# A prefix log-sum-exp kernel: half of its DMAs move from SyncE's queue to ScalarE's, and the last tile gets a stream of its own

## The chip, the cores and the metric

The kernel runs on one core of a Trainium2 chip. A core has five engines that run their own instruction streams and meet at semaphores: TensorE (PE in the profile; its weight loads are PEld), VectorE (DVE), ScalarE (ACT), GpSimd (POOL) and SyncE (SP). The data moves between HBM and the core's SBUF by 16 DMA engines, which an engine's instruction stream sets to work with a DMA instruction. The metric is the time of one execution on the device in microseconds (us); a lower time is better.

## The reference

For each of 4 batches and each of 4128 columns, a running log-sum-exp goes down 4096 rows:

```python
def setup_inputs():
    B, S, D = (4, 4096, 4128)
    return {'x': np.random.randn(B, S, D).astype(np.float32)}

def reference(x):
    B, S, D = x.shape
    out = np.zeros_like(x)
    out[:, 0, :] = x[:, 0, :].copy()
    for t in range(1, S):
        mx = np.maximum(out[:, t - 1, :], x[:, t, :])
        out[:, t, :] = mx + np.log(np.exp(out[:, t - 1, :] - mx) + np.exp(x[:, t, :] - mx))
    return out.astype(np.float32)
```

Row t of the output is log(exp(x[0]) + ... + exp(x[t])). All 270.5 MB of x are read once, and as many bytes of output are written.

## The kernel before, in words

**Tiles.** The rows of a batch are cut into tiles (class `Step`) of 128 x r rows and all 4128 columns. r is 3, but 32 blocks of 128 rows are not a multiple of 3, so one tile of each batch has r = 2: the first tile of batch 0, the last tile of the other three. That makes 11 tiles in each batch and 44 in all, numbered 0 to 43 here. Partition p of a tile holds r successive rows, so a tile of three rows is 128 x 12384 floats (6192 KB in the profile's DMA table), and one of two rows is 128 x 8256 (4128 KB). Tiles 0, 21, 32 and 43 are the small ones. Below, L43 is the load of tile 43 and S43 its store.

**Chunks.** A tile is computed in four chunks (class `Chunk`) of 1024 columns, and the last chunk carries the 32 columns that are left as a "tail" (tile `qt` in PSUM). For a chunk, ScalarE takes the exponential of all r rows at once (`exp`, line 142), in place, to fp16. TensorE then adds up along the partitions with triangular matrices (`head`, lines 92 and 96 through the helper `mm`): two matmuls with `incl` for row 0, two with `excl` for each further row, and, unless the tile is the first of its batch, two with `pick`, which add what the tile before has handed on in `carry`. `stage(j)` (line 175) takes the logarithm of the PSUM tile `pt` into row j of the tile (Ln), and two more matmuls with `ident` move `pt` on to row j + 1. After the last row `keep` (lines 106 and 107, VectorE) saves the carry of that chunk.

**Order.** The order of all instructions is written out by hand (`manual_schedule`). Iteration g of the main loop does the last stage of chunk g - 2, the middle stage of chunk g - 1 and the first of chunk g, then `exp` of chunk g + 2 and `head` of chunk g + 1. Chunks of successive tiles follow one another in this stream, so that `exp` for the first chunk of the next tile stands between the stages of the tile before.

**Buffers and DMAs.** Four tiles fit in SBUF (`xpool`, bufs = 4). The load (line 127) and the store (line 130) are issued by SyncE, whose stream has nothing else in it. When the last stage of tile k's last chunk has been done, SyncE issues S(k) and then L(k+3); that load goes into the buffer of tile k - 1 and waits until S(k-1) has landed. All DMAs lie in the one queue q1.

Of the kernel before, what the change touches and what calls it, by code (L numbers as in the profile page):

```python
# [11 lines left out]
R = 3  # L12
# [37 lines left out]
def kernel(  # L50
# [11 lines left out]
    nc = tc.nc  # L62
    B, S, D = x.shape
    assert S % P == 0
    n_main = D // CH
    tail = D - n_main * CH
    t0 = n_main * CH
    last = n_main - 1
# [5 lines left out]
    bufs = 4  # L74
# [37 lines left out]
    class Step:  # L112
# [7 lines left out]
            rows = t[self.b, self.row:self.row + P * self.r, :]  # L120
            return rows.rearrange("(p j) d -> p j d", j=self.r)

        def load(self):
            full = xpool.tile([P, R, D], FP32, name="xt")
            self.xt = full[:, :self.r, :]
            self.half = self.xt.bitcast(FP16)
            nc.sync.dma_start(out=self.xt, in_=self.dram(x))  # L127

        def store(self):
            nc.sync.dma_start(out=self.dram(out), in_=self.xt)  # L130

    class Chunk:
        def __init__(self, step, c):
# [51 lines left out]
    steps = []  # L185
# [8 lines left out]
            row += P * r  # L194
        assert row == S

    chunks = [Chunk(s, c) for s in steps for c in range(n_main)]
    ahead = bufs - 1
    for s in steps[:bufs]:
        s.load()  # L200
    stored = 0
    chunks[0].exp()
    chunks[1].exp()
    chunks[0].head()
    for g in range(len(chunks) + R - 1):
        for d in range(R - 1, -1, -1):
            if 0 <= g - d < len(chunks) and d < chunks[g - d].t.r:
                k = chunks[g - d]
                k.stage(d)
                if k.c == last and d + 1 == k.t.r:  # L210
                    k.t.store()
                    if bufs <= stored + ahead < len(steps):
                        steps[stored + ahead].load()
                    stored += 1
        if g + 2 < len(chunks):
            chunks[g + 2].exp()
        if g + 1 < len(chunks):
            chunks[g + 1].head()


# [28 lines left out]
```

## Time and profile before

| | |
|---|---|
| time, median of 3 runs | 1262.9 us (1262.69 to 1263.4) |
| span of the profiled execution, from its first to its last instruction | 1261.0 us |
| busy in that span: ACT / PE / DVE | 947.0 (75%) / 690.7 (55%) / 451.4 (36%) us |
| bytes moved, mean rate | 541.46 MB, 429 GB/s |
| share of the DMA engines' time in queue q1 | 99.4% |
| ScalarE's wait for loads (line 142) | 247.8 us, 42 times |

The profile is of one execution. Its span, 1261.0 us, is the execution's own time from first to last instruction; the measured times lie some 1.9 us above it. Busy times can overlap, since the engines work side by side; what bounds a kernel is read from the chain of work that ended last and from what each engine waited for. DMA-issuing instructions are not counted as busy. A DMA instruction's "time to landing" runs from its issue to the semaphore that reports that all of its bytes are there, so it includes the time in which the DMA stands in the queue behind others.

### The profile page before, as it was taken

What the parts mean: (1) busy time and instruction counts of PE and PEld (TensorE: products, weight loads), DVE (VectorE), ACT (ScalarE), POOL (GpSimd) and SP (SyncE); (2) the same over time, 40 slices, a digit from 0 to 9 for tenths busy, and PEclk for the clock granted to TensorE, in tenths of its full rate; (3) what the DMA queues carried; (4) which work ended last, traced back from release to release, by engine and by line L of the source; (5) the groups of instructions that cost most, each with busy time, mean ns of one, the idle gap of its engine ahead of it and who ended that gap; (6) DMA issues with size and microseconds to landing.
All of it is one profiled execution on the core that took longest, in us unless ns stands there. A gap on an engine that the chain in (4) does not pass through costs nothing.

```text
span 1261.0 us, 6165 instructions
## 1 busy us (share of the span) xinstructions
PE 690.7 (55%) x2268; PEld 236.3 (19%) x2268; DVE 451.4 (36%) x445; ACT 947.0 (75%) x733; POOL 2.2 (0%) x13
## 2 busy tenths in 40 slices
PE   3666545565565555555346655555534755555562
PEld 1222111121121111111112221211211211111120
DVE  2443333333333333334424333333442433333344
ACT  5997777777777777778569777777866977777784
POOL 0000000000000000000000000000000000000000
PEclk9987787877777777878778777777777778787776
DMA  9999999999999999999999999999999999999998
GB/s 411 411 443 428 432 429 437 431 431 434 437 429 431 431 439 431 434 427 434 436 431 433 434 431 438 430 434 432 435 431 433 437 430 434 433 434 431 433 420 348
DMA packets 12702, 541.46 MB, mean 429 GB/s; under 512 B 1408, under 2 KB 1408, under 8 KB 1408
## 3 DMA queue, kind: packets, MB, share of 16 engines
q1 hardware_dynamic: 12672, 541.07, 99.4%
q8 instruction: 18, 0.29, 0.1%
q14 instruction: 12, 0.10, 0.0%
HBM read 270.53 MB, written 270.53 MB: 429 GB/s over the span
## 4 chain that ended last, share of the span: by engine, by line
DMA 72%; ACT 19%; PE 5%; issue 2%; DVE 1%; SPq 0%; ACTq 0%
DMA xt<-in_x_dram 67%; ACT xt L142 10%; ACT xt L175 9%; DMA out_dram<-xt 5%; PE pt L96 3%; PE pt L92 2%; DVE carry L106 0%; DVE carry L107 0%; ACT xt L180 0%; SPq L130 0%; ACTq L244 0%; SPq L127 0%; ACTq L142 0%; PE qt L92 0%
## 5 line engine op out<-in xcount | busy, mean ns | idle before, releaser
L142 ACT ACTIVATE xt<-xt 128x3072 f16<-128x3072 f32 (+3 forms) x176 | 478.2, 2717 | 247.9 <-DMA xt<-in_x_dram 247.8
L175 ACT ACTIVATE xt<-pt 128x1024 f32<-128x1024 f32 x512 | 487.3, 1029 | 2.5 <-PE pt L96 0.7
L106 DVE CAST carry<-pt 32x1024 f16<-32x1024 f32 x176 | 216.5, 1230 | 760.9 <-ACT xt L175 760.7
L92 PE MATMUL pt<-xt,ident 128*128 128x512 f16 x176 | 76.6, 435 | 493.7 <-ACT xt L175 493.7
L96 PE MATMUL pt<-xt,ident 128*128 128x512 f16 x496 | 203.7, 477 | 35.4 <-ACT xt L175 34.7
L107 DVE TENSOR_TENSOR carry<-pt,carry 32x1024 f16<-32x1024 f32 x176 | 215.8, 1226 | 6.1
L96 PE MATMUL pt<-xt,excl 128*128 128x512 f16 x496 | 187.6, 496 | 0.0
L96 PEld LDWEIGHTS <-ident 128*128 128x128 f16 x496 | 51.0, 103 | 655.0 <-issue 641.3
L92 PE MATMUL pt<-xt,incl 128*128 128x512 f16 x176 | 92.2, 524 | 23.5 <-ACT xt L142 15.1
L92 PE MATMUL pt<-xt,excl 128*128 128x512 f16 x176 | 93.4, 531 | 0.0
L96 PE MATMUL pt<-xt,incl 128*128 128x512 f16 x176 | 92.9, 528 | 0.0
L96 PEld LDWEIGHTS <-excl 128*128 128x128 f16 x536 | 66.6, 124 | 104.1 <-issue 79.5
L92 PE MATMUL pt<-carry,pick 128*128 128x512 f16 x160 | 72.0, 450 | 0.0
L96 PE MATMUL pt<-carry,pick 128*128 128x512 f16 x160 | 68.5, 428 | 0.0
L180 ACT ACTIVATE xt<-qt 128x96 f32<-128x96 f32 (+1 forms) x44 | 10.9, 248 | 46.3 <-PE pt L96 46.3
L92 PEld LDWEIGHTS <-incl 128*128 128x128 f16 x220 | 22.6, 103 | 118.0 <-DVE carry L107 95.3
L92 PEld LDWEIGHTS <-excl 128*128 128x128 f16 x220 | 26.8, 122 | 36.8 <-issue 27.9
L96 PEld LDWEIGHTS <-incl 128*128 128x128 f16 x260 | 27.8, 115 | 10.9 <-issue 4.8
L92 PEld LDWEIGHTS <-pick 128*128 128x128 f16 x200 | 22.9, 114 | 30.4 <-issue 20.4
L96 PEld LDWEIGHTS <-pick 128*128 128x128 f16 x160 | 18.4, 115 | 28.6 <-issue 17.2
L92 PEld LDWEIGHTS <-ident 128*128 128x128 f16 x176 | 19.2, 109 | 22.7 <-issue 12.8
L106 DVE CAST carry_t<-qt 32x32 f16<-32x32 f32 x44 | 8.7, 197 | 26.0 <-ACT xt L180 25.8
(21 smaller groups left out, 56.5 us busy)
## 6 DMA issues: line engine op xcount, KB each, us to landing
xt<-in_x_dram SPq DMA_DIRECT2D x40, 6192.0 KB, 42.2
out_dram<-xt SPq DMA_DIRECT2D x40, 6192.0 KB, 28.1
xt<-in_x_dram SPq DMA_DIRECT2D x4, 4128.0 KB, 37.3
out_dram<-xt SPq DMA_DIRECT2D x4, 4128.0 KB, 29.6
```

What stands on the lines that cost most here:

```text
L92: nc.tensor.matmul(pt, lhsT=w, rhs=rhs, start=start, stop=stop, skip_group_check=True)
L96: pe.add_instruction(mybir.InstMatmult(name=nc.get_next_instruction_name(), ins=[pe.lower_ap(rhs), pe.lower_ap(w, for_matmul_weights=True) ...
L106: nc.vector.tensor_copy(cr[HI:HI + 32, :], pt[HI:HI + 32])
L107: nc.vector.tensor_tensor(out=cr[LO:LO + 32, :], in0=pt[HI:HI + 32], in1=cr[HI:HI + 32, :], op=mybir.AluOpType.subtract,)
L142: nc.scalar.activation(self.t.half[:, :, 2 * c0:2 * c0 + w], self.t.xt[:, :, c0:c0 + w], ACT.Exp,)
L175: nc.scalar.activation(t.xt[:, j, c * CH:(c + 1) * CH], pt, ACT.Ln)
L180: nc.scalar.activation(t.xt[:, :, t0:D], self.qt, ACT.Ln)
```

## The change

Three things change. (1) `load` and `store` are given the queue on which they are issued. Stores of tiles 0 to 21 and the loads that follow them (up to L24) are issued by SyncE as before; stores of tiles 22 to 43 and loads L25 to L43 are issued by ScalarE, out of the same instruction stream as its `exp` and Ln. (2) On ScalarE the load L(k+3) isn't issued right after S(k) but two iterations of the main loop later (`due[g + 2]`); it comes after the stages of that iteration and before its `exp`. On SyncE it stays in the same iteration. (3) The main loop runs twice: over the chunks of tiles 0 to 42 first, to the end of their last stages, and then over the four chunks of tile 43, which thus no longer stand between the stages of tile 42.

```diff
+        def load(self, queue):
...
-            nc.sync.dma_start(out=self.xt, in_=self.dram(x))
-
-        def store(self):
-            nc.sync.dma_start(out=self.dram(out), in_=self.xt)
+            queue.dma_start(out=self.xt, in_=self.dram(x))
+
+        def store(self, queue):
+            queue.dma_start(out=self.dram(out), in_=self.xt)
...
+    half = len(steps) // 2
+    stored = 0
+    due = {}
+    queue = lambda: nc.sync if stored < half else nc.scalar
     for s in steps[:bufs]:
-        s.load()
...
+        s.load(nc.sync)
+
+    for run in (steps[:-1], steps[-1:]):
+        chunks = [Chunk(s, c) for s in run for c in range(n_main)]
+        chunks[0].exp()
+        chunks[1].exp()
+        chunks[0].head()
+        for g in range(len(chunks) + R - 1):
+            for d in range(R - 1, -1, -1):
+                if 0 <= g - d < len(chunks) and d < chunks[g - d].t.r:
+                    k = chunks[g - d]
+                    k.stage(d)
+                    if k.c == last and d + 1 == k.t.r:
+                        k.t.store(queue())
+                        if bufs <= stored + ahead < len(steps):
+                            due[g if stored < half else g + 2] = (steps[stored + ahead], queue())
+                        stored += 1
+            if g in due:
+                s, q = due.pop(g)
+                s.load(q)
+            if g + 2 < len(chunks):
+                chunks[g + 2].exp()
+            if g + 1 < len(chunks):
+                chunks[g + 1].head()
+    assert not due
```

The removed loop is the same with `k.t.store()` and, right after it, `steps[stored + ahead].load()`, over the chunks of all tiles at once.

More of the change, by code (lines that the diff above doesn't have):

```diff
@@ L121, in dram @@
             return rows.rearrange("(p j) d -> p j d", j=self.r)
-        def load(self):
+        def load(self, queue):
             full = xpool.tile([P, R, D], FP32, name="xt")
@@ L195 @@
         assert row == S
-    chunks = [Chunk(s, c) for s in steps for c in range(n_main)]
     ahead = bufs - 1
+    half = len(steps) // 2
+    stored = 0
+    due = {}
+    queue = lambda: nc.sync if stored < half else nc.scalar
     for s in steps[:bufs]:
-        s.load()
[L201 to L218, printed above, removed]
+        s.load(nc.sync)
[22 more added lines that the diff above has]
+    assert not due
 _INS = ['x']
```

## The prediction

> **What bounds the kernel now.** I read the page first: the slices, the queues, the chain of work that ended last.
>
> ```profile
> DMA  9999999999999999999999999999999999999998
> q1 hardware_dynamic: 12672, 541.07, 99.4%
> DMA 72%; ACT 19%; PE 5%; issue 2%; DVE 1%; SPq 0%; ACTq 0%
> L142 ACT ACTIVATE xt<-xt 128x3072 f16<-128x3072 f32 (+3 forms) x176 | 478.2, 2717 | 247.9 <-DMA xt<-in_x_dram 247.8
> ```
>
> The DMA engines are busy in every slice, and ScalarE, the busiest compute engine, waits 247.8 us for loads: about 5.6 us in each of 44 tiles. The kernel is bound by its DMAs, and one queue suffices. Next, the DMA share by stretches; the last two columns are share and GB/s:
>
> ```profile
> 1180.00:1210.00 30.00, 16.53 (x56) 5.66 (x55) 10.21 (x10) 22.70 (x18) 0.00 (x0) 0.79 1.00 430
> 1226.00:1228.00 2.00, 2.00 (x7) 0.76 (x6) 0.46 (x3) 1.53 (x2) 0.00 (x0) 0.50 0.80 347
> 1228.00:1230.00 2.00, 0.68 (x3) 0.18 (x2) 0.54 (x1) 2.00 (x3) 0.00 (x0) 0.94 0.57 248
> 1230.00:1232.00 2.00, 1.28 (x4) 0.29 (x3) 1.92 (x2) 2.00 (x3) 0.00 (x0) 0.91 0.29 124
> 1232.00:1234.00 2.00, 2.00 (x6) 0.73 (x6) 0.00 (x0) 2.00 (x3) 0.00 (x0) 0.50 0.09 33
> 1234.00:1236.00 2.00, 0.89 (x3) 0.25 (x2) 1.96 (x2) 2.00 (x3) 0.00 (x0) 0.74 0.93 396
> ```
>
> In the steady part nothing is left (1.00). The only hole is at the end: S41 runs out engine by engine from 1226 to 1234, and S42 comes only then; 2 x (0.20 + 0.43 + 0.71 + 0.91 + 0.07) = 4.6 us of all engines. The timeline of SyncE dates S42 and S43, that of ScalarE the last tile, whose first `exp` starts when L43 has landed:
>
> ```profile
> 1234.00 0.33 SPq L130 DMA_DIRECT2D out_dram<-xt  x1
> 1244.51 0.33 SPq L130 DMA_DIRECT2D out_dram<-xt  x1
> ...
> 1216.53 2.86 ACT L175 ACTIVATE xt<-pt 128x1024 f32<-128x1024 f32 x3
> 1220.72 1.91 ACT L142 ACTIVATE xt<-xt 128x2048 f16<-128x2048 f32 x1 [1.34 <-DMA xt<-in_x_dram]
> 1243.46 1.02 ACT L175 ACTIVATE xt<-pt 128x1024 f32<-128x1024 f32 x1
> ```
>
> **Part 1: 22 stores and 19 loads issued by ScalarE.** On SyncE they cost 0.33 us and 0.38 us: 22 x 0.33 + 19 x 0.38 = 14.5 us, spread over 22 tiles, 0.7 us each. The wait for loads (5.6 us a tile) hides it, except for the last three (L43, S41, S42), after which ScalarE has no idle time to give: 1.0 us on the path. ScalarE's rows have no DMA issue; the bounds are 0.33 and the longest on SyncE, 1.5 us. I take SyncE's usual values: it is the same instruction. SyncE's queue loses what followed S21; nobody waits behind it.
>
> **Part 2: the loads two iterations later.** Stores land after 28.1 us (median) and tiles are 29.3 us apart, so when L(k+3) comes up S(k-1) has landed, and ScalarE does not block on it. L(k+3) now stands behind ScalarE's wait for L(k+2), then one `exp`, three Ln and the small Ln: by ScalarE's rows around L24's landing, 677.02 to 683.45, 6.4 us. In that time the DMA engines have S(k), which takes 14.65 us (half of 29.3). 8.2 us of it are left, so the queue never empties. The small tile 32 shortens its store to 9.75 us; its following load is issued before ScalarE's wait, since its last stage comes an iteration earlier. Cost in the steady part: nothing; the cover is the store ahead in the queue, and if it were gone each load would bring a gap of some 6 us.
>
> **Part 3: the change of queue.** S22 (668.50) goes to a new queue while L24 still runs in the old one (issued 638.10, 38.8 us to landing: 676.9). Before, S22 came behind it; now both have data at once. L24 lands later, ScalarE waits for it, and L25 stands behind that wait. S22 landed 23.1 us after issue, at 691.6; the last byte moves some 1.8 us earlier (S42, alone in the queue, took 16.4 us to landing, 14.65 of them transfer), at 689.8. L25 must be issued by 689.0 at the latest to start then (S42's bytes move from about 0.8 us after issue), so L24 must land by 682.6. If S22 were wholly first, L24 would land at 691.6: a gap of 9 us. If L24 keeps its place, none. With equal shares from 669.3 the 5.8 us of L24 that are left (to 675.1) take 11.6: it lands at 682.7, a gap of 0.1. Between 0 and 9 I take 0.5, as equal shares are nearest to a queue that all engines serve alike.
>
> No row shows two queues with data at once. The Trainium skill ("DMA: Bandwidth & Descriptors", section "Queues, rings and completion order") says that each engine takes turns between the queues that have work, a packet at a time. By that alone the gap would be the 0.1 us of equal shares, and the sum 0.4 us lower; no run here shows it yet.
>
> **Part 4: the last tile in its own stream.** Before, ScalarE ended three Ln at 1219.39 and went on with the last tile, interleaved with the stages that were left of tile 42. Now those come first. ScalarE reaches this point 0.71 us later (L43, S41): 1220.1. Then: two Ln and the wait for the last chunk's `head` (2.1 us of matmuls, 1220.13 to 1222.24 before) 2.85; its Ln 1.02; the wait before the small Ln 1.10 and itself 0.15; two Ln 1.95; two `ident` matmuls 0.9; the last Ln 1.02; S42's issue 0.4. Sum 9.4: S42 leaves at about 1229.1, 4.9 us earlier, but tile 43 begins at 1229.5, 8.8 us later than 1220.72. L43 has long landed.
>
> How long does tile 43 take alone? The nearest row is tile 0, the other two-row tile that runs by itself:
>
> ```profile
> 13.13 3.85 ACT L142 ACTIVATE xt<-xt 128x2048 f16<-128x2048 f32 x2 [11.05 <-DMA xt<-in_x_dram]
> 16.99 1.02 ACT L175 ACTIVATE xt<-pt 128x1024 f32<-128x1024 f32 x1
> ...
> 18.07 0.59 PE L92 MATMUL pt<-xt,ident 128*128 128x512 f16 x1 [1.11 <-ACT xt L175]
> 18.45 0.63 PE L96 MATMUL pt<-xt,ident 128*128 128x512 f16 x1
> ```
>
> Its matmuls start 0.43 us apart, half speed (0.22 in fast stretches, as at 1240). Tile 0 has no `pick`; tile 43 has two more matmuls per chunk. First Ln: 16.99 - 13.13 + 0.85 + 1.02 = 5.75. Then, per chunk, 0.06 + 7 x 0.43 + 0.63 + 0.02 + 1.02 = 4.75, three times; the small matmuls 0.25; at the end `ident`, small Ln and Ln 2.3: 22.55 us. At full speed ScalarE sets the pace: 4.9, twice 3.8, 3.2, 1.8: 17.5. I take 22.05: half speed as in tile 0, with only the last matmuls fast after the longest run of them.
>
> The Trainium skill ("TensorE: Matmul & The Clock Gate", Part 1) lets the clock double after a window of about 3.4 us of sustained work. The runs here would be 3.6 us with gaps of 1.1, so by that rule the clock could rise after any of them, and the stream take about 19.5 to 22: a sum up to 2.5 us lower than mine.
>
> So S43 is issued at 1229.5 + 22.05 + 0.05 = 1251.6 (1244.51 before). By then S42 is through (S41 landed at 1235.6, 14.65 more: 1250.2), so S43 runs alone: S42's 16.4 less a third of the transfer, 4.9: 11.5; landed 1263.1. From S43's landing (1244.51 + 15.7 = 1260.2) to the end the span had 0.8 more: 1263.9. With part 3: **1264.4** against the span of 1261.0. The measured median lies 1.9 above this span: **1266.3 us**, 0.27% slower.
>
> **Rivals.**
> *No measurable change.* The last tile's clock rises early: S43 at 1229.1 + 17.5 + 0.05 = 1246.6. Then the DMAs set the end: S42 through at 1250.2, S43 9.75 more, 0.8: 1260.8, with part 3 1261.3, time 1263.2. Up to 21.1 us for the stream the time stays under 1265.4. For it: TensorE ran fast in 1236 to 1244. Against it: that stretch had interleaved work; tile 0 had none and stayed slow.
> *The change of queue stalls* (slower): S22 goes first, 9 us more: 1275. It decides from about 2.5 us on. Against it: nothing here favours one queue.
> *Faster.* The hole of 4.6 us is filled, since S42 comes before S41 has run out: 1258.3. It needs S43 by 1245, that is, a stream of 15.5 us, below my full-speed sum, and that engines which finish S41 early set the end; the last one, at 1234, had no hole.
>
> **How the numbers follow.** A measurement of this kernel tells about 0.2% (2.5 us) from no change. Chances: forecast 0.45 (1265.4 to 1268), no change 0.40 (1262.5 to 1265.4), stall 0.09, faster 0.06; slower together 0.54. The range goes from the DMA bound, 1262.3, to 1270: the full 22.55, and issues on ScalarE at 1.5 us for the last three (3.5 more).
>
> **What would show it.** Part 1: DMA rows on ACT's queue near 0.35 us; ScalarE's waits for loads shorter by about 0.7 us a tile in the second half. Part 2: DMA share 1.00 from 700 to 1220; loads land some 23 us after issue (29.3 - 6.4) instead of 42.2. Part 3: one long wait of ScalarE, 5 to 8 us, near 677, and at most a short dip in DMA share near 690. Part 4: S42 near 1229, first `exp` of tile 43 just after it, S43 near 1251, no hole at 1228 to 1234 but one of 1 to 3 us before S43. I am wrong if the steady share falls below 0.99, if the dip at 690 exceeds 3 us, or if the last stream takes under 20 us.

## The result and the profile after

The changed kernel takes 1265.79 us (median of 13 runs, 1264.95 to 1266.52), the kernel before 1262.85 us in the same series (13 runs, 1262.45 to 1263.4): 2.9 us more, a ratio of 1.0023 with a 95% interval of 1.0015 to 1.0031. The forecast was 1266.3. The profiled execution has a span of 1263.6 us and a time of 1265.36, a little under the median.

The page of the changed kernel shows the two queues and a weak spot in the middle; the 22nd and 23rd of the GB/s slices are 404 and 414, and the DMA line's tenths don't show it:

```profile
span 1263.6 us, 6086 instructions
DMA  9999999999999999999999999999999999999998
GB/s 410 412 439 432 428 436 430 434 430 436 427 436 433 436 427 436 434 430 435 429 432 404 414 435 427 430 435 433 432 430 434 430 435 434 429 437 433 429 435 362
q1 hardware_dynamic: 6768, 289.56, 53.2%
q10 hardware_dynamic: 5904, 251.51, 46.3%
```

The table by stretches (last two columns: DMA share, GB/s) puts it at the change of queue. The first fence is of the kernel before, the second of the changed one:

```profile
686.00:694.00 8.00, 5.18 (x14) 1.73 (x14) 3.98 (x4) 8.00 (x8) 0.00 (x0) 0.79 0.98 423
700.00:1220.00 520.00, 288.51 (x947) 98.45 (x946) 184.33 (x181) 391.20 (x302) 0.00 (x0) 0.77 1.00 433
1226.00:1236.00 10.00, 6.85 (x19) 2.21 (x18) 4.88 (x7) 9.53 (x10) 0.00 (x0) 0.72 0.54 230
```

```profile
686.00:694.00 8.00, 4.92 (x13) 1.62 (x13) 3.83 (x5) 6.75 (x7) 0.00 (x0) 0.67 0.69 262
700.00:1220.00 520.00, 289.23 (x957) 101.42 (x956) 184.75 (x181) 399.27 (x305) 0.00 (x0) 0.78 1.00 431
1226.00:1236.00 10.00, 3.79 (x10) 1.12 (x9) 5.30 (x6) 7.49 (x7) 0.00 (x0) 0.73 0.95 411
```

At 686 to 694 the engines move 262 GB/s instead of the 431 of the steady part: 8 x (1 - 262/431) = 3.1 us are lost. In the 520 us after it, with all DMAs on ScalarE, the share is 1.00 as before (431 GB/s against 433). At the end the hole of 1226 to 1236 is gone, as S42 now waits in the queue; yet the time didn't fall.

ScalarE's timeline at the change of queue, in the changed kernel, shows how the gap comes about:

```profile
668.23 0.38 ACTq L130 DMA_DIRECT2D out_dram<-xt  x1
682.31 2.76 ACT L142 ACTIVATE xt<-xt 128x3072 f16<-128x3072 f32 x1 [6.09 <-DMA xt<-in_x_dram]
684.98 2.83 ACT L175 ACTIVATE xt<-pt 128x1024 f32<-128x1024 f32 x3
688.91 0.25 ACT L180 ACTIVATE xt<-qt 128x96 f32<-128x96 f32 x1 [1.10 <-PE pt L96]
688.91 0.35 ACTq L127 DMA_DIRECT2D xt<-in_x_dram  x1
```

S22 goes out at 668.23 on the new queue. ScalarE then waits 6.09 us for L24, which lands at 682.2 instead of 676.9; `exp`, three Ln and the small Ln follow, and only then L25 is issued, at 688.91. S22 landed 23.1 us after its issue, at 691.4.

And the end, in the changed kernel (ScalarE's timeline):

```profile
1198.05 2.76 ACT L142 ACTIVATE xt<-xt 128x3072 f16<-128x3072 f32 x1 [5.30 <-DMA xt<-in_x_dram]
1230.33 0.34 ACTq L130 DMA_DIRECT2D out_dram<-xt  x1
1230.71 3.85 ACT L142 ACTIVATE xt<-xt 128x2048 f16<-128x2048 f32 x2 [0.41 <-ACT xt L175]
1248.78 1.02 ACT L175 ACTIVATE xt<-pt 128x1024 f32<-128x1024 f32 x1
1249.83 0.34 ACTq L130 DMA_DIRECT2D out_dram<-xt  x1
```

L42's tile starts at 1198.05, 1.9 us later than before: two thirds of the whole loss are there before the last tiles begin. Tile 43 alone took 1249.83 - 1230.71 = 19.1 us. S42 needed 22.8 us to land (at 1253.1), S43 13.0 (at 1262.8): 9.7 us apart, the bare transfer of a small tile. By the trace's single packets the engines finished S42 one after another, from 1248.2 to 1252.6, and S43's first packets came at 1250.7. On the engines that were last S43 so still stood behind S42: there the DMAs set the end, not ScalarE.

### The profile page after: what moved, and what is told of

It is laid out like the page before. It is cut to its first block, busy times and chain, and to the rows that moved or that the text cites. A ratio compares the mean times of both kernels' runs of the same rounds, so it can differ in the third digit from the quotient of the medians.

```text
span 1263.6 us, 6086 instructions
## 1 busy us (share of the span) xinstructions
PE 688.2 (54%) x2268; PEld 239.0 (19%) x2268; DVE 451.4 (36%) x445; ACT 951.7 (75%) x733; POOL 2.2 (0%) x13
## 4 chain that ended last, share of the span: by engine, by line
DMA 71%; ACT 20%; PE 6%; issue 1%; DVE 1%; SPq 0%; ACTq 0%
DMA xt<-in_x_dram 69%; ACT xt L142 11%; ACT xt L175 9%; PE pt L96 4%; DMA out_dram<-xt 2%; PE pt L92 2%; ACT xt L180 0%; DVE carry L106 0%; DVE carry L107 0%; SPq L130 0%; ACTq L130 0%; SPq L127 0%; ACTq L127 0%; ACTq L142 0%; PE qt L92 0%
## 5 line engine op out<-in xcount | busy, mean ns | idle before, releaser
L92 PE MATMUL pt<-xt,ident 128*128 128x512 f16 x176 | 78.3, 445 | 499.0 <-ACT xt L175 498.8
L96 PE MATMUL pt<-xt,ident 128*128 128x512 f16 x496 | 205.2, 482 | 36.7 <-ACT xt L175 36.5
L107 DVE TENSOR_TENSOR carry<-pt,carry 32x1024 f16<-32x1024 f32 x176 | 215.8, 1226 | 6.1
## 6 DMA issues: line engine op xcount, KB each, us to landing
xt<-in_x_dram SPq DMA_DIRECT2D x23, 6192.0 KB, 42.2
xt<-in_x_dram ACTq DMA_DIRECT2D x17, 6192.0 KB, 22.7
```

What stands on the lines that cost most here:

```text
L92: nc.tensor.matmul(pt, lhsT=w, rhs=rhs, start=start, stop=stop, skip_group_check=True)
L96: pe.add_instruction(mybir.InstMatmult(name=nc.get_next_instruction_name(), ins=[pe.lower_ap(rhs), pe.lower_ap(w, for_matmul_weights=True) ...
L107: nc.vector.tensor_tensor(out=cr[LO:LO + 32, :], in0=pt[HI:HI + 32], in1=cr[HI:HI + 32, :], op=mybir.AluOpType.subtract,)
```

## The experiments

Two causes were possible in the changed kernel: the change of queue and the last stream. A third reading was a small price on each issue by ScalarE. All differences below are between medians, against runs of the kernel before on the same chip (1262.8 to 1262.9 us), unless another kernel is named.

**1. The change of queue alone.** Against the changed kernel:

```diff
-    for run in (steps[:-1], steps[-1:]):
+    for run in (steps,):
```

> The queue changes at tile 22 as in the change, but tile 43 stays in one stream with the others. Theory G (a gap at the change of queue: L24 and S22 share the engines, ScalarE waits for L24, and L25 stands behind that wait): 1.5 to 2.8 us above the kernel before, with the DMA share under 0.6 between 686 and 690 us and 1.00 from 700 us on. Theory P (each issue on ScalarE costs a little, 2.9 us / 22 tiles = 0.13 us a tile): 2.9 us, and no dip. Theory T (the last tile's own stream costs it): 0.

Measured: 1265.89 us, +3.0 us (ratio 1.0023, interval 1.0014 to 1.0032). Its table by stretches (last columns: DMA share, GB/s):

```profile
686.00:694.00 8.00, 4.71 (x13) 1.58 (x13) 3.84 (x5) 6.75 (x7) 0.00 (x0) 0.71 0.68 250
700.00:1220.00 520.00, 288.20 (x957) 101.16 (x956) 184.75 (x181) 398.89 (x305) 0.00 (x0) 0.78 1.00 432
```

8 x (1 - 250/431) = 3.4 us lost there; from 700 us on the share is 1.00. The whole loss of the change is in its queue part. It is a little above what theory G gave (1.5 to 2.8), and the share of 686 to 690 was 0.65, where under 0.6 was expected.

**2. The last stream alone.** Against the changed kernel:

```diff
-    queue = lambda: nc.sync if stored < half else nc.scalar
+    queue = lambda: nc.sync
...
-                            due[g if stored < half else g + 2] = (steps[stored + ahead], queue())
+                            due[g] = (steps[stored + ahead], queue())
```

> All DMAs on SyncE as before; only tile 43 has its own stream. Theory G: 0 to 1.2 us above the kernel before, as S43 is issued late (near 1248 us) but stands behind S42 in the queue anyway. Theory P: 0. Theory T: about 2.9 us, with a hole in the DMA share just before S43.

Measured: 1262.83 us, 0.0 us (ratio 1.0001, 0.9992 to 1.0010). S42 left at 1228.2 and landed 22.4 us later, at 1250.6; S43 left at 1248.0 and landed 12.3 us later, at 1260.3, 9.8 after S42. The hole only moved, from before S42 to before S43: the DMA share of 1226 to 1236 rose from 0.54 to 0.95, and that of 1236 to 1250 fell from 1.01 to 0.71. Theory T falls with this run, and theory P, which had no dip, with the first.

**3. L25 ahead of the wait.** Against kernel 1:

```diff
-                            due[g if stored < half else g + 2] = (steps[stored + ahead], queue())
+                            due[g if stored <= half else g + 2] = (steps[stored + ahead], queue())
```

> As the kernel that changes the queue alone, but L25, the first load on ScalarE's queue, is issued in the same iteration as S22, ahead of ScalarE's wait for L24; all later loads keep their two iterations. Theory G: the gap goes, -0.3 to 0.8 us against the kernel before, though L24 still lands some 6 us late. Theory P: still 2.9 us. A third reading, that sharing the engines between two queues itself wastes time: still about 2 us.

Measured: 1262.91 us, +0.05 us (1.0000, 0.9991 to 1.0009). ScalarE's timeline of this kernel, then a stretch with its DMA share:

```profile
668.58 0.38 ACTq L130 DMA_DIRECT2D out_dram<-xt  x1
669.06 3.79 ACTq L127 DMA_DIRECT2D xt<-in_x_dram  x1
682.64 2.76 ACT L142 ACTIVATE xt<-xt 128x3072 f16<-128x3072 f32 x1 [4.01 <-DMA xt<-in_x_dram]
```

```profile
686.00:694.00 8.00, 5.20 (x12) 1.63 (x12) 3.75 (x5) 6.90 (x8) 0.00 (x0) 0.61 1.00 429
```

L24 lands as late as in kernel 1 (682.6), and the engines are full: to within the interval, about 1.1 us either way, sharing them between two queues costs nothing in itself, and the whole loss goes with the gap behind ScalarE's wait.

**4. All DMAs on ScalarE.** Kernel 1 with `nc.scalar` for every load and store and `due[g + 2]` throughout.

> All DMAs on ScalarE's queue from the first load on, all loads two iterations later, one stream of chunks: no change of queue in flight. Theory G: only the activation table's load (1.28 us), which stands ahead of the first load on ScalarE, is lost: 0.9 to 1.7 us above the kernel before, and tiles 29.3 us apart. Theory P: that and 41 loads and 44 stores at half of 0.13 us each, 5.5 us more: about 6.9 us.

Measured: 1262.54 us, -0.3 us (0.9997, 0.9988 to 1.0006): not different. No price per issue shows; for all 88 together it is under 0.8 us by the interval. The 1.3 us at the start weren't lost either, a miss of mine; ScalarE's timeline there:

```profile
0.80 1.28 ACT L70 ACT_TABLE_LOAD   x1 [0.80 <-PEq L242]
0.84 1.94 ACTq L127 DMA_DIRECT2D xt<-in_x_dram  x4
```

The loads go out while the table load runs. Loads landed 22.8 us after issue in this kernel (42.2 before), and nothing was lost by that.

**5. The change of queue at tile 16.** Kernel 1 with another place:

```diff
-    half = len(steps) // 2
+    half = 16
```

> As the kernel that changes the queue alone (3.0 us above the kernel before), but at tile 16, far from a small tile. S16 then finds nearly all of L18 still to come: issued at 496.1, bytes from 496.9, L18's last byte 1.8 us before its landing at 509.9, so 11.2 us are left. Theory G with equal shares: L18 lands at 496.9 + 22.4 + 1.8 = 521.1, L19 is issued 6.6 us later and moves from 528.5, S16's bytes are through at 522.7: a gap of 5.8 us. 5.5 to 7.5 us above the kernel before. Rival (the first use of a second queue has a fixed price): 3.0 us again.

Measured: 1269.88 us, +7.1 us (1.0057, 1.0044 to 1.0069), inside theory G's range and far from the rival's. ScalarE's timeline of this kernel, then a stretch with its DMA share:

```profile
496.31 0.38 ACTq L130 DMA_DIRECT2D out_dram<-xt  x1
520.71 2.76 ACT L142 ACTIVATE xt<-xt 128x3072 f16<-128x3072 f32 x1 [16.41 <-DMA xt<-in_x_dram]
527.32 0.35 ACTq L127 DMA_DIRECT2D xt<-in_x_dram  x1
```

```profile
518.00:528.00 10.00, 2.65 (x7) 0.85 (x7) 2.83 (x4) 6.04 (x6) 0.00 (x0) 0.50 0.31 134
```

L18 landed at 520.7 (expected from equal shares: 521.1). 10 x (1 - 134/431) = 6.9 us are lost. By this theory tile 22, behind the small tile 21, was a cheap place: at S22's issue L24 was 8.7 us from the landing that it had before, L18 at S16's 13.6.

**6. L25 later still.** Kernel 1 with `g + 3` for that one load:

```diff
-due[g if stored < half else g + 2]
+due[g if stored < half else g + 3 if stored == half else g + 2]
```

> As the kernel that changes the queue alone, at tile 22, but L25 alone is issued three iterations after S22 instead of two. An iteration of ScalarE takes 5.4 us there. Theory G: 5.4 us more than with two iterations, 8.4 us above the kernel before (7.5 to 9.0). Rival (fixed price): 3.0 us.

Measured: 1268.09 us (1267.34 to 1270.43), +5.3 us (1.0045, 1.0032 to 1.0057). 8.4 was expected; the miss is in how far the issue moved. ScalarE's timeline of this kernel:

```profile
689.17 2.75 ACT L142 ACTIVATE xt<-xt 128x3072 f16<-128x3072 f32 x1
691.29 0.35 ACTq L127 DMA_DIRECT2D xt<-in_x_dram  x1
691.83 2.84 ACT L175 ACTIVATE xt<-pt 128x1024 f32<-128x1024 f32 x3
```

L25 left at 691.29, 2.4 us later than in kernel 1 (688.87) and not 5.4: it went out while the `exp` of 689.17 was running and before the three Ln that stand ahead of it in the program. For 2.4 us of delay the time rose by 1268.09 - 1265.89 = 2.2 us.

**7. The queues the other way round.** Kernel 1 with ScalarE first (`due[g + 2]`) and SyncE from S22 on (`due[g]`):

> The queues the other way round: ScalarE issues up to tile 21, SyncE the rest, one stream of chunks. The queue changes at the same place, but L25 stands on SyncE, which has nothing else to wait for. Theory G: no gap, -0.5 to 0.5 us against the kernel before, though L24 lands some 5 us late. Rival (fixed price of a change of queue): 3.0 us.

Measured: 1263.35 us, +0.5 us (1.0006, 0.9997 to 1.0015), at the edge of what was expected and not clear of no change. L24 landed at 682.3, L25 was issued on SyncE at 668.83, and 686 to 694 ran at 429 GB/s. A change of queue as such has no price near 3 us.

**8. A longer last stream.** Kernel 2, with the Ln of tile 43's second row done twice (the second writes the same values again):

```diff
-            nc.scalar.activation(t.xt[:, j, c * CH:(c + 1) * CH], pt, ACT.Ln)
+            for _ in range(2 if t is steps[-1] and j else 1):
+                nc.scalar.activation(t.xt[:, j, c * CH:(c + 1) * CH], pt, ACT.Ln)
```

> All DMAs on SyncE and tile 43 in its own stream, the four Ln of its second row done twice: up to 4 us more in the stream, some of it in ScalarE's waits for matmuls (2.6 us). S43 comes 1.5 to 4 us later than the 1248.0 of the kernel with the stream alone, where it just met the end of S42 (landed 1250.6, last byte about 1248.8). It then finds an empty queue: 1.0 to 4 us above that kernel. If there were slack behind S42: 0.

Measured: 1264.16 us (1262.99 to 1265.91), +1.3 us against kernel 2. S43 left at 1250.63 in the profiled run, 2.6 us later than in kernel 2, and landed 11.1 us after; S42 had landed at 1250.3. So S43 does become the bound once it is issued later than about 1248; the stream of the change lies at that edge.

**9. The change, with L25 ahead of the wait**, as in 3:

> The change as it is, with the last tile's own stream, but L25 issued in the same iteration as S22, ahead of ScalarE's wait for L24. Theory G, with the last stream free of cost: -0.5 to 0.5 us against the kernel before, and DMA share 0.95 or more in 686 to 694. If the last stream costs something once the gap is gone: about 1 us or more.

Measured: 1263.38 us (1262.54 to 1264.49), +0.6 us (1.0004, 0.9995 to 1.0013); the DMA share of 686 to 694 was 1.00. Without the gap S42 landed at 1250.3 and S43, issued at 1250.8, found an empty queue (11.1 us to landing; the profiled execution took 1264.4 us, 1 us above the median). What is left, if it is not noise, is probably this; no run shows it by itself.

**10. The change of queue at tile 16, with L19 ahead of the wait:**

> The change of queue at tile 16 (7.1 us above the kernel before), with L19 issued in the same iteration as S16. Theory G: the gap before L19 goes. L18 still lands at about 520.7, some 11 us late, so S17, behind it in ScalarE's stream by 16 us, is issued near 536.8 and moves from 537.6, where L19, behind S16 (through at 522.7), ends at 537.3 on the last engine and some 2 us earlier on the mean one: 0.5 to 2.5 us above the kernel before. Rival (the late landing itself costs): still 5 us or more.

Measured: 1264.34 us, +1.5 us (1.0013, 1.0004 to 1.0022), as expected. L18 lands just as late (520.8), S17 left at 536.61, and the stretch up to it, 528 to 536, is thin. The kernel's table there:

```profile
518.00:528.00 10.00, 2.59 (x7) 0.77 (x7) 2.77 (x4) 6.13 (x6) 0.00 (x0) 0.50 1.04 451
528.00:536.00 8.00, 6.17 (x18) 2.06 (x17) 2.54 (x3) 8.00 (x6) 0.00 (x0) 0.71 0.90 390
```

No kernel beat the one before beyond its interval.

## Why the prediction was right, and where it was not

The time (1266.3 against 1265.79), the sign and the size were right. Their make-up was not: the change of queue had 0.5 us and cost 3.0, the last stream had 2.9 and cost 0.0. That the sum came out is luck: two errors, one too small by 2.5 us and one too large by 2.9, cancelled. Two of the prediction's own signs of being wrong came true as well: the dip at 690 was 3.1 us by the table (limit 3), and the last stream took 19.1 us (limit 20).

**Part 1 was right.** The DMA rows on ScalarE's queue are 0.34 to 0.38 us long, and its waits for loads absorb them: in 700 to 1195 they fell from 102.1 to 85.8 us, 17 waits each, 1.0 us a tile where 0.7 was forecast. Kernel 4 shows no price either.

**Part 2 was right.** DMA share 1.00 from 700 to 1220; loads landed 22.7 us after issue (23 forecast).

**Part 3 named the mechanism and mis-sized it.** L24's landing by equal shares was forecast at 682.7 and came at 682.2. L25 left 6.7 us after it, at 688.9, where 689.0 was the limit worked out. By this the gap was 0.1, and I took 0.5; it cost 3.0 (kernel 1). The step that failed is the end of S22: I took its last byte on the last engine, 689.8, as the moment from which time is lost. The trace's single packets of the changed kernel tell what happened instead. The engines finished S22 one after another, from 686.4 to 690.9, and most of them then stood idle until L25's first bytes at 689.9, 1.0 us after its issue; and those first packets, on all engines at once, took 1.9 to 2.9 us instead of 1.83. Over the 16 engines this makes 2.1 us of idle time in the mean and 0.75 us of slow packets, 2.8 us in all.

So the loss is read from the bytes not moved, over all engines, and this agrees with the time to about half a microsecond: 3.1 us by the table and 2.9 by the clock in the changed kernel, 3.4 and 3.0 in kernel 1, 6.9 and 7.1 in kernel 5, 0.0 and 0.05 in kernel 3; in kernel 10 it is 0.8 and 1.5. Why the engines that were idle early could not make it up, though the last one had hardly waited, isn't shown by a run of its own.

The agreement hides one thing. In the profiled executions S41 landed only 1.6 us later than before in the changed kernel (1237.1 against 1235.6) and 2.2 us later in kernel 1 (1237.7); the last 0.9 to 1.1 us came behind it. There one engine carried a packet of 16 KB of queue q8, which the page calls "instruction": 1.08 us long, at 1240.2 in the changed kernel and at 1236.9 in kernel 1, with a packet of 2.22 us after it. In both this left a single engine 1.1 us behind all others at the end of S43. In the kernel before, the q8 packet (at 1233.1) fell into the hole ahead of S42. No run separates the two, so the price of the gap by itself may be nearer 2 us than 3 at this place.

The Trainium skill's rule of turns between queues ("DMA: Bandwidth & Descriptors", section "Queues, rings and completion order") agrees with the runs: 682.2 and 520.7 for the two late loads, 682.7 and 521.1 by equal shares. The packets show the turns themselves: on the engine that ended L24 last, one packet of each queue follows one of the other from 670.8 to 681.7. That the landing was met to 0.5 us is luck in part, since the working was wrong at both ends: S22's first packet came 3.5 us after its issue and not 0.8, and the landing comes 0.5 us after the last byte (S22: 690.9 and 691.4) and not 1.8. The 1.8 was S42's time beyond its transfer, start and end together.

**Part 4 was wrong in its term, S43 at 1251.6 and then alone.** It gave +2.9 us; kernel 2 shows 0.0, and in the changed kernel S43 didn't run alone on the engines that were last. The sum to the start of tile 43 was right: 33.4 us after L42's tile forecast, 32.7 measured. But tile 43 took 19.1 us and not 22.05, since the matmuls became fast in the middle (PE's timeline of the changed kernel):

```profile
1232.67 0.59 PE L92 MATMUL pt<-xt,incl 128*128 128x512 f16 x1 [3.43 <-ACT xt L142]
1236.50 0.58 PE L92 MATMUL pt<-xt,ident 128*128 128x512 f16 x1 [1.11 <-ACT xt L175]
1241.18 0.38 PE L92 MATMUL pt<-xt,ident 128*128 128x512 f16 x1 [1.11 <-ACT xt L175]
```

From start to start the matmuls take 0.43 us in the first two runs and 0.22 from the third on, half speed and then full speed: tile 0 was the wrong row to go by; its runs are of four and six matmuls and not of six and eight, though no run here shows that this is the reason. In the kernel before, the clock also rose only behind a longer run: ten matmuls at half speed from 32.37 to 36.8, full speed from 38.17. The sentence on the skill's clock gate ("TensorE: Matmul & The Clock Gate", Part 1) had 19.5 to 22 for it, just above the 19.1 measured. And S42's delay gave S43 cover: S42 landed 2.7 us later than before (1253.1 against 1250.4), and S43 was issued at 1249.8, before S42 was through on its last engines.

**The rivals.** "No measurable change" had the end right (the DMAs set it) and the change of queue wrong. "The change of queue stalls" had the right place, at three times the size, and the wrong cause: S22 didn't go first, or L24 would have landed at 691.6 and not at 682.2. "Faster" failed as its condition said: S43 came at 1249.8 and not by 1245, and kernel 2 shows that filling the hole before S42 only opens one before S43.

## What to carry to other kernels

When the DMA engines are full, as here, it mattered little which engine issued the transfers, but a hand-over from one queue to another did: the transfers that still run in the old queue share the engines with the new one and land later, and whatever is issued behind a wait for them comes late as well. Issue the next transfer ahead of that wait, and estimate the cost from the bytes not moved by all engines in that stretch; from the last engine alone it came out as almost nothing here. A hole in the DMAs at the end of a kernel is worth something only if what comes after it can come earlier too.

## What the runs showed of the hardware

Four things I had not expected. A DMA instruction on ScalarE didn't wait for the work ahead of it to end: it went out at 0.84 beside a table load of 0.80 to 2.08, and at 691.29 beside an `exp` of 689.17 to 691.9 and ahead of Ln that begin at 691.83. A load issued on ScalarE's queue right behind a store, with another transfer still running in SyncE's queue, held ScalarE for 3.79 us in kernel 3 and 4.10 in kernel 9 (0.35 otherwise), but 0.35 at tile 16 in kernel 10; what it waited for isn't known. A queue that starts while another keeps the engines full gets its first packet late: S22's came 3.5 to 5.0 us after its issue, engine by engine. And a load on empty engines starts slowly: L25's first bytes came 1.0 us after its issue, and its first packets took 1.9 to 2.9 us instead of 1.83, while the store S42 in the kernel before, on empty engines as well, began after 0.8 us with packets of 1.85 to 1.88.
